# Final-norm column factors on VectorE instead of GpSimd, and a separate early buffer for the plain weights of the last product

## The chip, the cores and the metric

The kernel runs on one core of one Trainium2 chip. The metric is the device time of the whole program in microseconds (us), the median over several runs. A profile of one execution stands beside it; its span is the time from the first to the last instruction, and all moments named below are us from the start of that span.

## The reference, cut to what matters

One layer of a hybrid encoder on 528 tokens (512 real ones and 16 prepended) of width 2048, all in float32. `hn = rmsnorm(h) * g_in`; `P = hn @ w_in` (2048 x 8320); half of the columns feed an RWKV-7 recurrence, the other half a gated short convolution; the two results, 1024 wide each, are joined to `mix`. Then

```python
h_res = h_res + mix @ w_out[l]          # 512 x 2048 by 2048 x 2048
out = _rmsnorm(h_res, norm_f_g)         # h * rsqrt(mean(h*h) + eps) * norm_f_g
return out[:, N_META:]
```

The change lies wholly in these last lines: the product with `w_out`, the sum with `h_res`, and the final norm with its 2048 column factors `norm_f_g`.

## The kernel before, in words

**Numbers.** TensorE multiplies in a reduced float32 form, so each operand is split in two: ScalarE casts it to a high part (`hi`, L1215 for weights of the last stage), VectorE subtracts that from the plain value to get the low part (`lo`, L1216), and each product is the sum of three matmuls, `hi*hi`, `lo*hi` and `hi*lo`.

**Stages.** The first 842 us hold the input projection and the recurrence. Then TensorE runs the last stage, the product with `w_out`, and nothing else. The 2048 output columns are two halves of 1024, and each half is computed by a scheme with seven block products instead of eight: `M1`, `M2`, `P5`, `M7`, `M3`, `Q6`, `P4`. Sums of weight blocks and of activation blocks (`S1`, `S3`, `S4`, `S5`) are formed ahead of them, partly on VectorE (`add`, L1206; `sums`) and partly by transfers that add to what lies in memory (`add_by_transfer`, L1202, issued on GpSimd's queue). Each product is cut in four units g = 0 to 3 along the inner dimension; a unit is twelve matmuls of 128x512 (two token tiles, two inner slices, three matmuls each). The 56 units stand in the list `units`: `M1` and `M2` of the first half are units 0 to 7, its four blocks of `P5 M7 M3 Q6` are 8 to 23, then `P4` and the second half's `M1` up to 31, the second half's four blocks 32 to 47, its `P4` 48 to 51, its `M2` 52 to 55. The last four units, those of the second half's `M2`, run with the tail in a block of their own (the accumulators `end`).

**Order.** TensorE's order is written out. For the other engines, `at(u, fn, ...)` hangs a piece of work on unit u, and it is handed to the scheduler just before the matmuls of that unit; the scheduler then fixes each engine's own order, and every engine works its list strictly in that order. Only the tail block (from `row_part`) has VectorE, ScalarE and GpSimd in hand-written order. Buffers rotate: split weights `o` go through 6 half-unit slots (three units' worth), plain weights `wo` through 3 buffers (tag `raw`, loaded by `request`, L1148, on SyncE's queue SP), and a load into a buffer waits until its last reader is done. `x` are four standing buffers, one for each g, in which weight sums build up.

**After a product** comes `close`: VectorE adds the accumulators onto the output rows, which lie in `xa` (columns 0 to 1023) and `xb` (columns 1024 to 2047) on top of the residual (`onto`, L1224), and ScalarE squares the finished ones (`squares`, L1230).

**The two pieces that the change touches.** `gain` (L1299 to L1301) multiplies a finished 128x512 piece by its column factors, loaded to `gfb`. For columns 0 to 1023 that is eight pieces: four token tiles t, two column pieces n. They run on GpSimd, hung on units 30, 32, ..., 44. `load_home(g)` (L1304) fetches the plain weights of the second half's `M2`, unit g, through the three rotating `raw` buffers (hung on units 41, 43, 45, 47), and splits them into tiles called `home`, which lie where the activation sums `S` lay before. The mixed activations themselves (`mix`, four quarters with the tags `R0` to `R3`) are finished with once the sums are split; `R0` then takes `gfb`, `R2` and `R3` take `xb`, and `R1` stays unused.

Of the kernel before, what the change touches and what calls it, by code (L numbers as in the profile page):

```python
# [9 lines left out]
F32 = mybir.dt.float32  # L10
# [8 lines left out]
P = 128  # L19
# [58 lines left out]
def hymba_kernel(ctx: ExitStack, tc: tile.TileContext, xt, xtok, front, w_in, w_out, pv, lup, cst, msk, gf, out):  # L78
    nc = tc.nc
# [539 lines left out]
    def behind(dst, src):  # L619
        with tc.issue_after(state["dma"]):  # L620
            nc.sync.dma_start(dst, src)
# [450 lines left out]
    pp = ctx.enter_context(tc.tile_pool(name="pp", bufs=1, side="right", reuse_waits="tile"))  # L1072
# [70 lines left out]
    def rows_of(half, k, col, g):  # L1143
        return w_out[2 * half + col, 4 * k + g]

    def request(half, k, col, g):
        t = wp.tile([P, 1024], F32, tag="raw", name=f"wo{half}{k}{col}{g}", bufs=3)
        state["dma"] = nc.sync.dma_start(t, rows_of(half, k, col, g)).ins  # L1148
        straight[half, k, col, g] = t
# [58 lines left out]
    def split_unit(unit, t, home=None):  # L1208
        for q in range(2):
            rq = t()[:, q * 512 : (q + 1) * 512]  # L1210
            if home is None:
                hi, lo = slot(f"o{U[unit]}_{q}", OUT_AT)
            else:
                hi, lo = home[q]
            nc.scalar.copy(hi, rq)  # L1215
            nc.vector.tensor_tensor(out=lo, in0=rq, in1=hi.bitcast(F32), op=ALU.subtract)  # L1216
            right[unit, q] = (hi, lo)
# [64 lines left out]
    def at(u, fn, *args):  # L1282
        calls.setdefault(max(u, -1), []).append((fn, args))
# [17 lines left out]
        eng.tensor_tensor(out=h, in0=h, in1=gfs[0][:, n * 512 : (n + 1) * 512][:, o], op=ALU.mult)  # L1301


    def load_home(g):  # L1304
        request(1, 1, 0, g)
        f = ("S1", "S3", "S4", "S5")[g]
        tiles = [
            pw.tile([P, 4, HT], F32R, tag=f"{f}0{a}", name=f"home{g}{a}").rearrange("p a b -> p (a b)") for a in range(2)
        ]
        split_unit(  # L1310
            (1, "M2", g), passing(1, 1, 0, g),
            [(tiles[0][:, 512 * q : 512 * q + 512], tiles[1][:, 512 * q : 512 * q + 512]) for q in range(2)],
        )

    def passing(*block):
        return lambda: straight[block]

    def chained(g):
        return lambda: chain[g]
# [3 lines left out]
    for half in range(2):  # L1323
        for g in range(4):
            b, m1, m2 = U[half, "P5", g], U[half, "M1", g], U[half, "M2", g]
            if half:
                at(m1 - 4, begin_chain, 1, g)
                at(m1 - 2, split_unit, (1, "M1", g), chained(g))
            at(max(m1 + (half == 0 and g == 3), b - 5), add_by_transfer, half, 0, 1, g)
            at(b - (6 if g else 5), request, half, 0, 1, g)  # L1330
            at(b - (4 if g else 5), request, half, 1, 1, g)
            at(b - 2, split_unit, (half, "P5", g), chained(g))
            at(b - 1, add, passing(half, 0, 1, g), half, 1, 1, g)
            at(b - 1, split_unit, (half, "M7", g), passing(half, 0, 1, g))
            at(b, split_unit, (half, "M3", g), passing(half, 1, 1, g))
            at(b, add, chained(g), half, 1, 1, g)
            at(b + 1, split_unit, (half, "Q6", g), chained(g))
            at(b + 2, add_by_transfer, half, 1, 0, g)
            at(U[half, "P4", g] - 2, split_unit, (half, "P4", g), chained(g))
            if half:  # L1340
                at(m2 + 2 * g - g - 11, load_home, g)
            else:
                at(m2 - 5, request, 0, 1, 0, g)
                at(m2 - 2, split_unit, (0, "M2", g), passing(0, 1, 0, g))
# [6 lines left out]
    at(13, load_gain)  # L1351
    for m in range(2):
        at(21 + m, load_xb, m)
    for n in range(8):
        at(30 + 2 * n, gain, n // 2, n % 2, nc.gpsimd)

    for e in range(6):
        right[(0, "M1", e // 2), e % 2] = quarters[2 * N_IN + e]
# [5 lines left out]
    for u, unit in enumerate(units):  # L1364
        half, prod, g = unit
# [152 lines left out]
```

## Time and profile before

| | us |
|---|---|
| median of 3 runs (lowest, highest) | 1010.39 (1008.97, 1011.24) |
| the profiled execution | 1008.48 |
| its span | 1006.6 |
| last stage, from its first matmul on | 842.18 |
| first unit of the second half's blocks (`P5`, unit 32) starts | 929.07 |
| first matmul of the second half's `M2` (unit 52) starts | 987.03 |
| last matmul ends | 998.38 |

The profiled execution is 1.91 us below the median; of its own 1008.48 us, 1.9 lie outside the span. How to read the rows: PE is TensorE, DVE VectorE, ACT ScalarE, POOL GpSimd, and SPq, POOLq, ACTq their queues. A timeline row gives the start, the duration, the engine, the source line, the operation with output and inputs, and how many like it were merged (x4); in brackets the idle time just ahead of the row and what ended it. Consecutive instructions of one engine overlap by some 0.1 us, so of a merged row the duration divided by the count is the pace.

### The profile page before, as it was taken

The numbers are of one execution on the slowest core, as the hardware profiler recorded it, in microseconds if no ns is written. First come the engines' busy times: TensorE is split into PE (matmuls) and PEld (weight loads), VectorE is DVE, ScalarE is ACT, GpSimd is POOL, SyncE is SP. The second block draws the span as 40 slices with busy tenths as digits, with TensorE's granted clock in tenths as the row PEclk, the third lists the DMA queues.
The fourth block names the chain that finished last, engine by engine and source line by source line (L and its number), as shares of the span: only waits on it lengthen the run. The fifth ranks groups of instructions, "written<-read, shape, count | busy, mean of one in ns | idle before, by whom it ended". The sixth has DMA issues, their size and how long they took to land.

```text
span 1006.6 us, 23759 instructions
## 1 busy us (share of the span) xinstructions
PE 993.2 (99%) x9723; PEld 912.7 (91%) x9723; DVE 683.2 (68%) x1305; ACT 393.0 (39%) x729; POOL 288.0 (29%) x294
## 2 busy tenths in 40 slices
PE   9999999999999999999999999999999999999996
PEld 8999998999998999998999998889888898888775
DVE  7686955587765668654668654244555697999787
ACT  7553423344313434322434322222222336546453
POOL 0123313224223423232323222223332333047001
PEclk9999999999999999999999999999999999999998
DMA  9526476446674363854273856977673688796754
GB/s 338 155 70 154 115 205 159 125 125 146 155 186 146 94 171 99 218 152 119 85 175 94 222 141 192 340 237 234 216 216 95 177 271 235 210 281 146 173 130 168
DMA packets 185181, 175.35 MB, mean 174 GB/s; under 512 B 121584, under 2 KB 142832, under 8 KB 184560
## 3 DMA queue, kind: packets, MB, share of 16 engines
q1 hardware_dynamic: 182480, 164.92, 56.9%
q0 software_dynamic: 2304, 8.39, 4.9%
q8 instruction: 76, 1.25, 0.5%
q10 hardware_dynamic: 288, 0.52, 0.1%
q14 instruction: 33, 0.27, 0.1%
HBM read 137.44 MB, written 36.35 MB: 173 GB/s over the span
## 4 chain that ended last, share of the span: by engine, by line
PE 62%; DVE 5%; DMA 2%; issue 2%; ACT 0%; POOL 0%; DVEq 0%; ACTq 0%; POOLq 0%
PE ps_gc L328 8%; PE ps_B L328 7%; PE ps_h L328 7%; PE ps_C L328 7%; PE ps_k L328 5%; PE ps_v L328 5%; PE M L1243 5%; PE ps_g L328 5%; PE ps_r L328 5%; DVE o L1216 2%; PE P L1243 2%; DMA wo<-in_w_out_dram 2%; PE Q L1243 1%; PE zy L1010 1%; PE zs L1006 1%
## 5 line engine op out<-in xcount | busy, mean ns | idle before, releaser
L135 POOL TENSOR_TENSOR w<-wr,w 128x512 fp32r<-128x512 f32 x119 | 166.8, 1403 | 365.8 <-ACT w L134 317.5
L134 ACT CAST w<-wr 128x512 fp32r<-128x512 f32 x252 | 152.9, 618 | 280.9 <-PE ps_k L328 45.2
L135 DVE TENSOR_TENSOR w<-wr,w 128x512 fp32r<-128x512 f32 x133 | 95.9, 728 | 103.6 <-ACT w L134 93.3
L328 PE MATMUL ps_k<-xh,w 128*128 128x256 f32 (+1 forms) x512 | 95.7, 284 | 0.1
L328 PE MATMUL ps_r<-xh,w 128*128 128x256 f32 (+1 forms) x512 | 95.1, 281 | 0.0
L328 PE MATMUL ps_v<-xh,w 128*128 128x272 f32 (+1 forms) x512 | 95.0, 283 | 0.0
L328 PE MATMUL ps_h<-xh,w 128*128 128x258 f32 (+1 forms) x512 | 94.0, 282 | 0.0
L328 PE MATMUL ps_C<-xh,w 128*128 128x258 f32 (+1 forms) x512 | 93.2, 281 | 0.0
L328 PE MATMUL ps_g<-xh,w 128*128 128x258 f32 (+1 forms) x512 | 91.9, 281 | 0.0
L328 PE MATMUL ps_B<-xh,w 128*128 128x512 f32 x256 | 83.4, 395 | 0.1
L328 PE MATMUL ps_gc<-xh,w 128*128 128x512 f32 x256 | 81.7, 393 | 0.3 <-DVE w L135 0.3
L328 PEld LDWEIGHTS ps_h<-xh,w 128*128 128x128 f32 x512 | 79.7, 189 | 2.3 <-issue 1.6
L328 PEld LDWEIGHTS ps_k<-xh,w 128*128 128x128 f32 x512 | 80.3, 189 | 0.7 <-DVE w L135 0.3
L328 PEld LDWEIGHTS ps_r<-xh,w 128*128 128x128 f32 x512 | 80.3, 189 | 0.2
L328 PEld LDWEIGHTS ps_v<-xh,w 128*128 128x128 f32 x512 | 80.0, 189 | 0.3
L328 PEld LDWEIGHTS ps_C<-xh,w 128*128 128x128 f32 x512 | 79.6, 189 | 0.6
L328 PEld LDWEIGHTS ps_g<-xh,w 128*128 128x128 f32 x512 | 79.3, 189 | 0.4
L328 PE MATMUL ps_k<-xl,w 128*128 128x272 f32 (+1 forms) x256 | 72.9, 285 | 0.0
L328 PE MATMUL ps_v<-xl,w 128*128 128x256 f32 (+1 forms) x256 | 72.5, 283 | 0.0
L328 PE MATMUL ps_r<-xl,w 128*128 128x256 f32 (+1 forms) x256 | 72.4, 283 | 0.0
L328 PE MATMUL ps_g<-xl,w 128*128 128x256 f32 (+1 forms) x256 | 72.3, 282 | 0.0
L328 PE MATMUL ps_C<-xl,w 128*128 128x256 f32 (+1 forms) x256 | 71.9, 281 | 0.0
(320 smaller groups left out, 2288.2 us busy)
## 6 DMA issues: line engine op xcount, KB each, us to landing
wr<-in_w_in_dram SPq DMA_DIRECT2D x126, 512.0 KB
ct<-opd SPq DMA_DIRECT2D x64, 288.0 KB
wo<-in_w_out_dram SPq DMA_DIRECT2D x25, 512.0 KB
x<-in_w_out_dram POOLq DMA_DIRECT2D x16, 512.0 KB, 5.7
opd<-ar SPq DMA_DIRECT2D x8, 576.0 KB
opd<-gt SPq DMA_DIRECT2D x16, 288.0 KB
opd<-bt SPq DMA_DIRECT2D x64, 64.0 KB
x<-in_w_out_dram SPq DMA_DIRECT2D x8, 512.0 KB
```

The lines of the kernel that those rows point to most:

```text
L134: nc.scalar.copy(hi, rq)
L135: low[q] = eng.tensor_tensor(out=lo, in0=rq, in1=hi.bitcast(F32), op=ALU.subtract).ins
L328: nc.tensor.matmul(ps[r], ww[:, w], xx[:, kt, a:b], start=(kt == 0 and n == 0), stop=(kt == KT - 1 and n == 2))
L1006: nc.tensor.matmul(d[hs, j], w, x[hs], start=(a == 0), stop=(a == b - 1))
L1010: nc.tensor.matmul(d[ho, j], t[hs, o : o + CH], x[hs], start=(a == 0), stop=(a == b - 1))
L1216: nc.vector.tensor_tensor(out=lo, in0=rq, in1=hi.bitcast(F32), op=ALU.subtract)
L1243: nc.tensor.matmul(bank[s], left(prod, jj, m, s), w, start=(jj == 0 and n == 0), stop=(jj == 7 and n == 2))
```

## The change

The eight `gain` calls go to VectorE and are hung on units 34, 35, 38, 39, 41, 42, 44 and 46. The plain weights of the second half's `M2` no longer pass through the rotating `raw` buffers: `fetch_home(0)` loads those of g = 0 and 1 into the unused quarter `R1` (hung on unit 23), `fetch_home(1)` those of g = 2 and 3 into the same quarter (hung on unit 44, and so once the first pair is split). `load_home` only splits; it is hung on units 40, 43, 47 and 48 instead of 41, 43, 45 and 47.

```diff
+    plain = {}
+
+    def fetch_home(pair):
+        t = pp.tile([P, 4, 512], F32, tag="R1", name=f"plain{pair}").rearrange("p a b -> p (a b)")
+        for g in (2 * pair, 2 * pair + 1):
+            plain[g] = t[:, g % 2 * 1024 : g % 2 * 1024 + 1024]
+            behind(plain[g], rows_of(1, 1, 0, g))
+
     def load_home(g):
-        request(1, 1, 0, g)
         f = ("S1", "S3", "S4", "S5")[g]
         tiles = [
             pw.tile([P, 4, HT], F32R, tag=f"{f}0{a}", name=f"home{g}{a}").rearrange("p a b -> p (a b)") for a in range(2)
         ]
         split_unit(
-            (1, "M2", g), passing(1, 1, 0, g),
+            (1, "M2", g), lambda: plain[g],
             [(tiles[0][:, 512 * q : 512 * q + 512], tiles[1][:, 512 * q : 512 * q + 512]) for q in range(2)],
         )
...
             if half:
-                at(m2 + 2 * g - g - 11, load_home, g)
+                at((40, 43, 47, 48)[g], load_home, g)
...
+    at(23, fetch_home, 0)
+    at(44, fetch_home, 1)
     for n in range(8):
-        at(30 + 2 * n, gain, n // 2, n % 2, nc.gpsimd)
+        at((34, 35, 38, 39, 41, 42, 44, 46)[n], gain, n // 2, n % 2, nc.vector)
```

In the built program, TensorE's list is the same. On VectorE the scheduler puts two of the eight gains ahead of the splits of unit 19, one between the splits of units 30 and 31, two behind those of unit 31, one behind those of unit 32, and the last two ahead of those of unit 35; the addition of two `wo` buffers that stood ahead of unit 35's splits now stands behind them. The `home` splits stand, half by half, between the splits of units 39, 40 and 41 (g = 0 and 1) and of units 43 to 46 (g = 2 and 3). Behind the last unit's splits, the four pairs of small sums over the squares (`row_part`) stand ahead of the last two additions of `P4` instead of behind them. GpSimd's list loses the eight gains and keeps its transfers in their order. On SP the first pair's two loads stand right behind those of `xb`, and the second pair's two loads are the last before the outputs.

## Prediction

> **What bounds the kernel now.** I read the chain of waits first, because it says which engine holds the end, then TensorE's timeline in the last stage, then that of the engine it waits for.
>
> ```profile
> span 1006.6 us, 23759 instructions
> ```
> ```profile
> 842.18 21.77 PE M L1243 x96
> ...
> 925.38 4.46 DVE o L1216
> ...
> 961.51 5.53 DMA wo<-in_w_out_dram
> ```
>
> Up to 918 us the chain names almost only PE, so nothing there can be won by moving work of other engines. One number is needed from it: 96 matmuls without a stop take 21.77 us, so a unit of twelve takes 2.721. Behind that the chain leaves PE for splits on VectorE (one of 4.46 us) and for weight loads. TensorE's timeline shows what these cost:
>
> ```profile
> 929.07 2.92 PE L1243 MATMUL P<-o,S 128*128 128x512 f32 x12
> ...
> 933.16 5.55 PE L1243 MATMUL M<-o,S 128*128 128x512 f32 x23 [0.95 <-DVE o L1216]
> ...
> 939.28 2.77 PE L1243 MATMUL Q<-o,S 128*128 128x512 f32 x11 [0.35 <-DVE o L1216]
> 941.89 2.88 PE L1243 MATMUL P<-o,S 128*128 128x512 f32 x12
> ...
> 969.67 2.82 PE L1243 MATMUL M<-o,S 128*128 128x512 f32 x11 [0.19 <-DVE o L1216]
> ...
> 981.68 5.51 PE L1243 MATMUL P<-o,m 128*128 128x512 f32 x23 [0.28 <-DVE o L1216]
> 987.03 5.60 PE L1243 MATMUL end<-home,m 128*128 128x512 f32 x24
> ```
>
> Four stops, each released by a low part `o` from VectorE. The brackets understate them, because a stop also loses the overlap of matmuls; the starts give the whole loss. Units 32 to 35 take 941.89 - 929.07 = 12.82 us instead of 4 x 2.721 = 10.88: 1.94 lost. Units 36 to 51 take 987.03 - 941.89 = 45.14 instead of 43.54: 1.60 lost. So 3.54 us is what this stage can give back.
>
> **Part 1, the eight gains.** What they do now, on GpSimd, and what VectorE does meanwhile:
>
> ```profile
> 883.93 8.89 POOL L1301 TENSOR_TENSOR xa<-xa,gfb 128x512 f32<-128x512 f32 x2 [0.52 <-DMA gfb<-in_gf_dram]
> ...
> 925.47 1.59 POOL L1301 TENSOR_TENSOR xa<-xa,gfb 128x512 f32<-128x512 f32 x1
> ...
> 927.32 1.90 POOL L1301 TENSOR_TENSOR xa<-xa,gfb 128x512 f32<-128x512 f32 x1
> ...
> 929.18 2.23 POOL L1301 TENSOR_TENSOR xa<-xa,gfb 128x512 f32<-128x512 f32 x1
> ...
> 940.24 0.90 POOL L1202 DMA_DIRECT2D x<-in_w_out_dram  x1 [8.82 <-DVE o L1216]
> ```
> ```profile
> 889.13 1.29 DVE L1216 TENSOR_TENSOR o<-x,o 128x512 fp32r<-128x512 f32 x2
> ...
> 917.91 1.22 DVE L1206 TENSOR_TENSOR wo<-wo,wo 128x1024 f32<-128x1024 f32 x1
> ...
> 924.00 5.83 DVE L1216 TENSOR_TENSOR o<-x,o 128x512 fp32r<-128x512 f32 x2 [0.25 <-ACT o L1215]
> 929.86 2.64 DVE L1206 TENSOR_TENSOR x<-x,wo 128x1024 f32<-128x1024 f32 x1
> 932.43 1.28 DVE L1216 TENSOR_TENSOR o<-wo,o 128x512 fp32r<-128x512 f32 x2
> ...
> 937.40 1.23 DVE L1206 TENSOR_TENSOR wo<-wo,wo 128x1024 f32<-128x1024 f32 x1 [1.29 <-DMA wo<-in_w_out_dram]
> 938.54 2.50 DVE L1216 TENSOR_TENSOR o<-x,o 128x512 fp32r<-128x512 f32 x4
> ...
> 995.54 0.68 DVE L1301 TENSOR_TENSOR xb<-xb,gfb 128x512 f32<-128x512 f32 x1
> ```
>
> A pair of splits takes 1.29 us at 889.13; the pair at 924.00 takes 5.83, just while three gains run on GpSimd. The addition at 929.86 takes 2.64 where the one at 917.91 takes 1.22. Excess 4.54 + 1.42 = 5.96 us. The next split, unit 33's (932.43), is the one TensorE stops for at 933.16.
>
> The Trainium skill ("SBUF — State Buffer", Who interferes with whom) says that a VectorE operation with two inputs in SBUF and a GpSimd operation that reads SBUF exclude each other for whole instructions. By it VectorE would have waited at most for the three gains, 1.59 + 1.90 + 2.23 = 5.72 us, beside 5.96 by VectorE's own rows; the sum comes out alike.
>
> Added on VectorE: the same operation stands there already, 0.68 us alone, and four in a row go at 2.50 / 4 = 0.62. Four of the gains now stand between the splits of unit 30 and those of unit 33: 4 x 0.62 = 2.48. So unit 33's splits start 5.96 - 2.48 = 3.5 us earlier, at about 928.9, and TensorE wants the low part at 929.07 + 2.72 + 0.23 = 932.0: it is there by 929.6, and the stop goes. If the contention were halved only, 3.0 - 2.5 would still bring it 0.5 earlier and leave about 0.6 of the stop. The last two gains stand ahead of unit 35's splits. These stop TensorE at 939.28 today, because VectorE first waits for a load until 937.40 for an addition; that addition now stands behind them, so 1.24 us of gains replace 2.4 us of waiting and adding, on a list that is 3.5 us early. Both stops of this stretch go: **-1.94**, bounds 0 and -1.94.
>
> The first two gains stand ahead of unit 19's splits, at 889.13 today. Their factors were there at 883.93, when GpSimd started on them, so VectorE doesn't wait. 1.24 us later unit 19's splits end at 891.7; TensorE starts that unit at 842.18 + 19 x 2.721 = 893.9. Cost nothing, hidden by these 2 us. GpSimd's transfers no longer queue behind gains, and come earlier; who waits for them is not late now, so no gain.
>
> **Part 2, the plain weights.** What VectorE and ScalarE do ahead of the two late stops:
>
> ```profile
> 967.06 1.14 ACT L1215 CAST home<-wo 128x512 fp32r<-128x512 f32 x2 [4.31 <-DMA wo<-in_w_out_dram]
> ...
> 979.20 1.14 ACT L1215 CAST o<-x 128x512 fp32r<-128x512 f32 x2 [2.37 <-DMA x<-in_w_out_dram]
> ```
> ```profile
> 967.72 1.29 DVE L1216 TENSOR_TENSOR home<-wo,home 128x512 fp32r<-128x512 f32 x2 [2.57 <-ACT home L1215]
> 968.93 1.29 DVE L1216 TENSOR_TENSOR o<-wo,o 128x512 fp32r<-128x512 f32 x2
> ...
> 977.34 1.29 DVE L1216 TENSOR_TENSOR home<-wo,home 128x512 fp32r<-128x512 f32 x2
> 978.55 2.47 DVE L1224 TENSOR_TENSOR xb<-xb,M 128x512 f32<-128x512 f32 x4
> 980.94 1.29 DVE L1216 TENSOR_TENSOR o<-x,o 128x512 fp32r<-128x512 f32 x2
> ```
> ```profile
> 942.00:962.00 20.00, 20.00 (x90) 16.58 (x89) 14.22 (x22) 9.35 (x17) 1.74 (x2) 1.00 0.60 156
> ...
> 976.00:987.00 11.00, 10.71 (x47) 8.55 (x46) 11.00 (x20) 1.97 (x4) 0.00 (x0) 1.00 0.20 38
> ```
>
> In the windows VectorE (third busy column) is idle for 5.8 of the 20 us from 942 on, and never from 976 to 987. A `home` load that came late held ScalarE 4.31 us and VectorE 2.57, and unit 46's split at 968.93, the stop at 969.67, waited behind them. The stop at 981.68 is unit 50's split at 980.94, behind the `home` pair at 977.34 and four additions. Now the first pair of loads is in memory long before, and all four `home` splits stand ahead of unit 46's last ones: VectorE does 4 x 1.24 us of them by about 963, in the stretch where it was idle. Behind 967 it has three pairs, 3.7 us, less to do, against losses of 1.60: **-1.60**, bounds 0 and -1.60.
>
> Two loads move past others on SP. The first pair, 1 MB, comes ahead of `wo` loads of the second half:
>
> ```profile
> 889.50 0.77 SPq L1148 DMA_DIRECT2D wo<-in_w_out_dram  x1
> ```
>
> At the 390 GB/s that the output rows below show, 1 MB delays what is behind it by 2.7 us; its first reader is the addition at 917.91, 28 us later. Nothing. The second pair needs its quarter free (g = 1 split, about 949) and the `wo` load ahead of it on SP issued, which waits for unit 41's splits, done at the latest when TensorE starts that unit: 929.07 + 9 x 2.721 = 953.6. With the slow 5.53 us load of the chain and 2 x 1.35 (0.52 MB at 390 GB/s) for the two behind it, the last lands at 961.8. ScalarE has its cast ahead of unit 45's, wanted at 929.07 + 13 x 2.721 = 964.4, less two casts of 0.6: 963.2. Hidden by 1.4 us in this worst count.
>
> **Part 3, the tail.** Reordered row sums: the four pairs now wait on ScalarE's squares ahead of the last two additions, but at a moment when VectorE has caught up, so nothing. Beside that:
>
> ```profile
> 993.06 0.34 SPq L1405 DMA_DIRECT2D out_dram<-xb  x1
> ```
> ```profile
> GB/s 0 0 0 0 0 0 0 0 0 289 429 410 386 366 395 376 386 366 419 429 414 366 424 424 347 400 371 376 390 362 400 376 386 386 198 19 0 0 0 0
> ```
>
> The second row covers 990 to 1007 in steps of 0.425 us: from the first output on, the transfers run full, some 390 GB/s, for 11 us until 1005. The first output starts when VectorE is done with all additions, 3.5 us behind the end of `P4` at 987; with VectorE no longer behind, it starts up to 2.5 us earlier against TensorE, and the last rows, released by TensorE's end, find a shorter queue. Between 0 and -0.5; I take **-0.3**.
>
> Sum: -1.94 - 1.60 - 0.3 = -3.84. Against the profiled execution, 1008.48, that gives 1004.6; the median of the runs shown is 1010.39, so 1006.5.
>
> **Rivals.**
>
> *Only the first stops go* (0.13). VectorE stays saturated behind 967, or the late stops come from the additions alone. For it: 11.00 busy of 11.00. Against: 3.7 us of `home` splits leave that stretch. -1.94: 1008.4.
>
> *The gains are not what slows VectorE* (0.06), but GpSimd's three transfer issues between them. Then the 5.96 stays and 2.48 comes on top; the stop at 939 (0.4) and the late ones (1.6) still go: +0.5, 1010.9. Against: the issue at 940.24 falls into the four splits at 938.54, which keep their 0.62.
>
> *The second pair lands late* (0.06), the case for slower. Place: ScalarE's cast ahead of unit 45's. From 963.2 on each us of lateness stops TensorE for one. If its loads went one behind the other at 5.53 each, the last would land at 953.6 + 16.6 = 970.2: +7.0 - 3.84 = +3.2, 1013.6. Against: full rate is 1.35 a load.
>
> *Accumulating transfers starve* (0.03). The last one for `P4`:
>
> ```profile
> 973.63 0.88 POOL L1202 DMA_DIRECT2D x<-in_w_out_dram  x1 [12.24 <-DVE o L1216]
> ...
> DMA to landing us min/median/max: 5.3/5.6/9.3
> ```
>
> If its issue had to wait for a pause in a VectorE that is now busy without one until about 982, it would land 5.6 later at 987.6; with cast and split at 988.8, for unit 51 at 929.07 + 19 x 2.721 = 980.8: +8.0 - 3.84 = +4.2, 1014.6. Against: issued at 973.63, it had landed at 979.20, in the middle of a busy VectorE.
> The Trainium skill ("SBUF — State Buffer", SBUF: two separate sides) describes such a starving of transfers issued on GpSimd by VectorE operations in a 2-port mode; by these rows it does not happen under this kernel's two-input ones.
>
> **How the numbers follow.** The forecast has 0.72. Range 1005.0 to 1010.0: below, -4.04 and the 1.4 by which the lowest run lies under the median; above, the first rival and that spread; left out are the last three, 0.15. Faster means by over 0.2% (2 us), about what a measurement of this kernel can tell from no change: forecast without its weak edge and half of the first rival, 0.74; within 0.2%: 0.17; slower: 0.09.
>
> **What would show it.** Right: splits of units 32 and 33 at 0.6 to 0.7 us each, no DVE release in PE's rows behind 929, `end` starting near 983.5, the first output near 987 to 990, no ScalarE wait on `home` loads. Wrong: a split of over 1 us with GpSimd idle; PE waiting at units 45 or 51 (late load, starved transfer); or all stops gone and the end not moved, if the outputs bound it.

## The result and the profile after

| | before | after |
|---|---|---|
| median (lowest to highest) of 8 runs, us | 1010.72 (1008.97 to 1013.59) | 1005.67 (1004.08 to 1009.29) |
| profiled execution, us | 1008.48 | 1006.95 |
| its span | 1006.6 | 1005.2 |
| last stage starts | 842.02 | 842.72 |
| unit 32 starts | 929.07 | 931.77 |
| tail block (`end`) starts | 987.03 | 986.17 |

The stage's first matmul row starts at 842.02; the 842.18 given ahead of the prediction is where the chain of waits enters the stage. The ratio is 0.9952, 95% interval [0.9937, 0.9966]: 5.05 us by the medians, against 3.84 forecast. The profiled execution of the changed kernel is 1.28 us above its own median, and its span is only 1.4 us shorter. So this one profile needs care. TensorE's timeline, from the first unit at which it stops, to the tail (start, duration, instruction, count, idle time before it and its releaser):

```profile
868.50 5.52 PE L1243 MATMUL M<-o,S 128*128 128x512 f32 x23 [0.43 <-DVE o L1216]
...
880.18 5.51 PE L1243 MATMUL M<-o,S 128*128 128x512 f32 x23 [0.16 <-DVE o L1216]
...
931.77 2.88 PE L1243 MATMUL P<-o,S 128*128 128x512 f32 x12
...
975.29 11.04 PE L1243 MATMUL P<-o,m 128*128 128x512 f32 x48
986.17 5.60 PE L1243 MATMUL end<-home,m 128*128 128x512 f32 x24
```

From unit 32 to the tail no bracket is left: 986.17 - 931.77 = 54.40 us for twenty units of 2.720, where the kernel before took 57.96. All 3.54 us that the forecast had counted there are gone. But two stops stand near units 9 and 13 (868.50 and 880.18), where instructions and order are the same in both kernels, and with them the first 32 units take 931.77 - 842.72 = 89.05 us instead of the 87.05 of before: 2.0 us of the gain are hidden in this execution. They come back below.

VectorE at the place of the old contention, and GpSimd there:

```profile
927.75 1.28 DVE L1301 TENSOR_TENSOR xa<-xa,gfb 128x512 f32<-128x512 f32 x2
928.95 1.28 DVE L1216 TENSOR_TENSOR o<-x,o 128x512 fp32r<-128x512 f32 x2
930.16 0.68 DVE L1301 TENSOR_TENSOR xa<-xa,gfb 128x512 f32<-128x512 f32 x1
930.76 1.22 DVE L1206 TENSOR_TENSOR x<-x,wo 128x1024 f32<-128x1024 f32 x1
931.89 1.28 DVE L1216 TENSOR_TENSOR o<-wo,o 128x512 fp32r<-128x512 f32 x2
```
```profile
928.23 0.89 POOL L1202 DMA_DIRECT2D x<-in_w_out_dram  x1 [2.13 <-DVE o L1216]
```

Pairs of splits take 1.28 us again, where a pair had taken 5.83, and a multiplication takes 0.68 alone and 0.64 in a pair. GpSimd's transfer issues still fall between them (928.23) and slow nothing. The long split of before, 4.46 us at 925.38, is one of 0.68 plus 3.78, and the two GpSimd multiplications that ran beside it took 1.59 + 1.90 = 3.49 by their rows. The Trainium skill ("SBUF — State Buffer", Who interferes with whom) says that the side which has the shared ports keeps them for its whole instruction, and that the other blocks fully meanwhile; the trace agrees to 0.3 us.

The `home` splits, and one wait that the forecast had not seen, on ScalarE:

```profile
914.52 2.19 ACT L1215 CAST o<-x 128x512 fp32r<-128x512 f32 x4 [3.69 <-DMA x<-in_w_out_dram]
...
960.03 0.62 ACT L1215 CAST home<-plain 128x512 fp32r<-128x512 f32 x1 [2.90 <-DMA plain<-in_w_out_dram]
```

The second pair landed at 960.0, when ScalarE had waited 2.90 us for it; VectorE's `home` halves, which stand between the splits of units 43, 44 and 45, follow at once, and no stop comes of it. The first pair's 1 MB pushed an `x` load of unit 27 back, so that its cast waited 3.69 us; TensorE did not stop for it. One window (its length, then busy us and count of PE, PEld, DVE, ACT, POOL):

```profile
962.00:976.00 14.00, 14.00 (x64) 11.58 (x63) 14.00 (x23) 8.21 (x15) 0.88 (x1) 1.00 0.47 70
```

VectorE is busy without a pause from 962 to 976, PE too: a full VectorE that is ahead costs nothing. The accumulating transfers did not starve under it:

```profile
DMA to landing us min/median/max: 5.1/5.8/9.8
```

### The profile page after: what moved, and what is told of

Its sections match the earlier page's. It is cut to its first block, busy times and chain, and to the rows that moved or that the text cites. A ratio compares the mean times of both kernels' runs of the same rounds, so it can differ in the third digit from the quotient of the medians.

```text
span 1005.2 us, 23750 instructions
## 1 busy us (share of the span) xinstructions
PE 993.7 (99%) x9723; PEld 913.6 (91%) x9723; DVE 680.5 (68%) x1313; ACT 393.2 (39%) x729; POOL 264.2 (26%) x286
## 3 DMA queue, kind: packets, MB, share of 16 engines
q8 instruction: 76, 1.25, 0.5%
## 4 chain that ended last, share of the span: by engine, by line
PE 65%; DVE 3%; DMA 1%; ACT 1%; SPq 0%; issue 0%; DVEq 0%; POOL 0%; ACTq 0%
PE ps_gc L328 8%; PE ps_B L328 7%; PE ps_h L328 7%; PE ps_C L328 6%; PE M L1243 5%; PE ps_k L328 5%; PE ps_v L328 5%; PE ps_g L328 5%; PE ps_r L328 5%; PE P L1243 4%; PE Q L1243 2%; PE zy L1010 1%; PE zs L1006 1%; PE g L681 1%; PE rz L954 1%; DVE o L1216 1%
```

## The experiments

All were measured against runs of the kernel before on the same chip. **Lost** below is read from each TensorE timeline: start of `end` less the first matmul of the last stage, less 141.46, which is the shortest such stretch (the changed kernel profiled again, 984.43 - 842.97). "Tail" is the span less the start of `end`.

| kernel | median us | ratio, 95% interval | lost up to unit 31 | lost in 32 to 51 | tail |
|---|---|---|---|---|---|
| before, first profile | | | 0 | 3.55 | 19.57 |
| whole, first profile | 1005.67 | 0.9952 [0.9937, 0.9966] | 1.99 | 0 | 19.03 |
| gains alone | 1005.43 | 0.9955 [0.9937, 0.9972] | 0 | 0.05 | 19.05 |
| homes alone | 1008.35 | 0.9981 [0.9969, 0.9993] | 2.06 | 1.40 | 19.37 |
| gains left out | 1006.53 | 0.9966 [0.9953, 0.9979] | 0.33 | 0.02 | 19.48 |
| whole, again | 1005.04 | 0.9949 [0.9934, 0.9965] | 0 | 0 | 18.97 |
| gains alone, doubled | 1006.45 | 0.9970 [0.9958, 0.9982] | 0 | 0.73 | 19.10 |
| whole, first pair later | 1004.78 | 0.9955 [0.9938, 0.9972] | 0.42 | 0 | 19.01 |
| whole, residual later | 1005.79 | 0.9962 [0.9948, 0.9976] | 0.42 | 0.02 | 19.24 |
| gains alone, residual later | 1005.48 | 0.9957 [0.9941, 0.9973] | 0 | 0 | 19.07 |
| whole, gains doubled | 1004.56 | 0.9944 [0.9929, 0.9960] | 0 | 0 | 19.02 |

### The two parts, each alone

The theory was the forecast's: two causes, one for each part. Its rival: one cause, GpSimd's multiplications, whose lateness is carried on to the late stops.

Gains alone is the kernel before with one edit:

```diff
-        at(30 + 2 * n, gain, n // 2, n % 2, nc.gpsimd)
+        at((34, 35, 38, 39, 41, 42, 44, 46)[n], gain, n // 2, n % 2, nc.vector)
```

> Only the eight column factors go to VectorE; the weights of the last product come through the rotating buffers as before. Theory (two separate causes): the two stops near 933 and 939 go, worth 1.9 us, the stops near 970 and 982 stay within 0.5 us of their 1.6: -1.5 to -2.5 us against the kernel before. Rival (one cause: VectorE, once ahead, stays ahead, and the late loads matter no more): all stops go, -3.5 to -5 us, as the whole change. Rival (VectorE is full and the gains only add to it): 0 or slower.

Measured: 1005.43 against 1009.49, 4.1 us by the medians and 4.5 by the ratio, nearly all of the whole change. TensorE's timeline of gains alone:

```profile
929.50 2.88 PE L1243 MATMUL P<-o,S 128*128 128x512 f32 x12
...
973.01 11.10 PE L1243 MATMUL P<-o,m 128*128 128x512 f32 x48
983.95 5.60 PE L1243 MATMUL end<-home,m 128*128 128x512 f32 x24
```

The stops of before at 969.67 and 981.68 are gone too, although the `home` weights still go through the rotating buffers. Only the 11.10 us of the last `P4`, 0.06 more than in the whole change, are left of them. The one-cause rival holds, and the theory falls.

Homes alone is the other part, with the gains left on GpSimd:

```diff
-        at((34, 35, 38, 39, 41, 42, 44, 46)[n], gain, n // 2, n % 2, nc.vector)
+        at(30 + 2 * n, gain, n // 2, n % 2, nc.gpsimd)
```

> Only the separate buffer and the earlier splits of the last product's weights; the eight column factors stay on GpSimd at their old places. Theory: the long split near 924 (5.8 us for two) and the stops near 933 and 939 stay, the two late stops go, and the first output leaves earlier: -1.5 to -2.2 us against before. Rival (one cause, the gains): nothing, within 0.7 us of before. Rival (the moved splits press on VectorE while GpSimd still holds it back): slower by 0.5 to 1.5 us.

Measured: 1008.35, by the ratio 1.9 us (0.7 to 3.1) below before, as the theory had it, but only 1.1 by the medians; its profile, of 1008.30 us, does not bear the theory's reason out. TensorE's timeline of homes alone, and ScalarE's cast ahead of the last stop:

```profile
925.40 3.73 PE L1243 MATMUL M<-o,m 128*128 128x512 f32 x15 [0.71 <-DVE o L1216]
...
929.35 2.14 PE L1243 MATMUL M<-o,m 128*128 128x512 f32 x8 [0.22 <-DVE o L1216]
931.33 2.89 PE L1243 MATMUL P<-o,S 128*128 128x512 f32 x12
...
965.85 2.11 PE L1243 MATMUL P<-o,S 128*128 128x512 f32 x8 [0.24 <-DVE o L1216]
```
```profile
962.65 0.62 ACT L1215 CAST home<-plain 128x512 fp32r<-128x512 f32 x1 [5.79 <-DMA plain<-in_w_out_dram]
```

The contention struck here before unit 32 and cost 2.06 us there, then 1.40 more, of which 1.24 from unit 44 on. The stops of before at units 46 and 50 are gone, but a new one stands in unit 44: VectorE does its split behind a `home` split of the second pair, and that pair landed only at 962.6. So the forecast's rival *The second pair lands late* came true in this kernel, by a stop. All in all it lost 3.46 us in this execution, hardly less than the 3.55 of before; where the 1.1 to 1.9 us come from, one profile doesn't show.

### Multiplications or transfer issues

Gains left out is the kernel before without its eight multiplications (so columns 0 to 1023 lack their factor), with all of GpSimd's transfers:

```diff
-    for n in range(8):
-        at(30 + 2 * n, gain, n // 2, n % 2, nc.gpsimd)
```

> The kernel before without the eight column factors at all (columns 0 to 1023 of the output lack the factor, so this is no result, only a time). Theory (GpSimd's multiplications hold VectorE's two-input operations): splits of units 32 and 33 take 0.6 to 0.7 us each, the stops near 933 and 939 go, and it comes within 0.5 us of the kernel that has only the gains moved, as VectorE's 2.5 us for them are hidden. Rival (GpSimd's three transfer issues in that stretch hold VectorE): the 5.8 us pair stays, no gain against before.

Measured: 54.42 us from unit 32 to the tail and no stop there. TensorE and VectorE of this kernel, where the pair of splits had taken 5.83:

```profile
929.60 2.88 PE L1243 MATMUL P<-o,S 128*128 128x512 f32 x12
...
984.02 5.60 PE L1243 MATMUL end<-home,m 128*128 128x512 f32 x24
```
```profile
924.33 1.38 DVE L1216 TENSOR_TENSOR o<-x,o 128x512 fp32r<-128x512 f32 x2 [0.83 <-ACT o L1215]
```

From 886 to 985 the operations of VectorE and of ScalarE come in the same order as in the kernel before. So the multiplications were the cause, of the late stops too, and the transfer issues were not. The median, 1006.53, is 1.1 above gains alone, not within 0.5 as expected, though the intervals overlap. Eight multiplications on VectorE cost nothing that can be seen.

The whole change once more beside these:

> The whole change once more beside its parts, on the same chip. Theory: no stop of TensorE behind unit 30, -3.8 to -5 us against before, and the sum of the two parts within 1 us. Rival (parts overlap): the whole is no better than the better part.

Measured: 1005.04, 4.45 below before. Its profiled execution took 1005.19. From that of before: 0.95 later start of the stage, 3.55 not lost, 0.60 less tail, 1008.48 + 0.95 - 3.55 - 0.60 = 1005.28. Whether the parts add up the times can't tell: alone they give 6.4 by the ratios beside 5.1 for both, over 1 us more, but 5.2 beside 4.45 by the medians. What can be said is that the whole change is not measurably better than gains alone (0.9949 and 0.9955), as the rival had it, and that by the profiles gains alone leave 0.05 us to win.

### Is VectorE full, and what does the separate buffer buy?

Each gain done twice (columns 0 to 1023 get the factor squared) adds 8 x 0.62 us on VectorE, first without the buffer:

```diff
+        for _ in range(2):
-        at((34, 35, 38, 39, 41, 42, 44, 46)[n], gain, n // 2, n % 2, nc.vector)
+            at((34, 35, 38, 39, 41, 42, 44, 46)[n], gain, n // 2, n % 2, nc.vector)
```

> Gains on VectorE without the separate buffer, and each of the eight multiplications done twice, so that columns 0 to 1023 carry the factor squared: eight more VectorE operations of 0.62 us, 4.96 us in all, with nothing on GpSimd. Of them some six stand between the splits of units 30 and 35. Theory, that a VectorE held up by GpSimd lost TensorE's time once and that the late stops were the same lateness carried on: in e1 the splits of unit 33 had about 1.8 us to spare; the second copies take up to 2.5 us there, so a stop of 0 to 0.7 us comes back near 932, well under the 1.94 of before, and what is late is made up in the 5.8 idle us of 942 to 962, so no late stop over 0.2 us. Against e1: 0 to +0.8 us. Rival, that VectorE is simply full in this stage and any addition moves the end by its length: +3 to +5 us against e1, with late stops as in the kernel before.

Measured: 1.0 us above gains alone by the medians, 1.5 by the ratios, a little more than the theory had, and 0.73 lost. The rival's 3 to 5 us did not come, so VectorE is not full; but the theory had the place wrong, and its "no late stop over 0.2 us" failed. The scheduler put the extra copies near unit 20 and behind unit 36's splits, so the stretch ahead of unit 33 wasn't loaded, and the stop came at unit 50. TensorE and VectorE of this kernel:

```profile
973.79 5.98 PE L1243 MATMUL P<-o,m 128*128 128x512 f32 x25
980.03 5.53 PE L1243 MATMUL P<-o,m 128*128 128x512 f32 x23 [0.26 <-DVE o L1216]
```
```profile
975.69 1.29 DVE L1216 TENSOR_TENSOR home<-wo,home 128x512 fp32r<-128x512 f32 x2
976.89 2.48 DVE L1224 TENSOR_TENSOR xb<-xb,M 128x512 f32<-128x512 f32 x4
979.28 1.30 DVE L1216 TENSOR_TENSOR o<-x,o 128x512 fp32r<-128x512 f32 x2
```

In gains alone that split starts at 977.74, and its first half is done 0.3 us before TensorE wants it (929.50 + 18 x 2.72 + 0.23 = 978.7). The separate buffer should turn this 0.3 into several us. The same doubling in the changed kernel:

> The whole change with each of the eight multiplications done twice, as in e5 (columns 0 to 1023 carry the factor squared). e5, without the separate buffer, lost 0.7 us between unit 32 and the tail, with a stop at unit 50, whose split was 0.3 us ahead of TensorE in e1 and 3.5 us ahead in the changed kernel. Theory, that the separate buffer buys time in hand at units 46 and 50, which is worth something only where VectorE is late: no stop behind unit 32, start of unit 32 to the start of the tail within 0.1 us of 54.42, and the time within 0.7 us of the changed kernel's, so 0.5 to 1.5 us below e5. Rival, that it buys nothing: the stop at unit 50 comes back and the time is e5's.

Measured: 1004.56 and nothing lost; 984.58 - 930.18 = 54.40. That is 1.9 us below the same doubling without the buffer, by the medians, more than the 0.5 to 1.5 expected; the lost 0.73 explains a part, and the rest stays open. TensorE's timeline and VectorE's split of unit 50:

```profile
930.18 2.88 PE L1243 MATMUL P<-o,S 128*128 128x512 f32 x12
...
973.70 11.04 PE L1243 MATMUL P<-o,m 128*128 128x512 f32 x48
984.58 5.60 PE L1243 MATMUL end<-home,m 128*128 128x512 f32 x24
```
```profile
973.93 1.32 DVE L1216 TENSOR_TENSOR o<-x,o 128x512 fp32r<-128x512 f32 x2
```

The first half is done at 974.6, wanted at 979.4: 4.8 us in hand. By one profile of each, part 2 buys time in hand that the gains alone don't need, but that twice the gains do.

### The first pair's traffic, and the early stops

The first pair of plain weights at unit 32 instead of 23:

```diff
-    at(23, fetch_home, 0)
+    at(32, fetch_home, 0)
```

> The whole change, with the first pair of plain weights fetched at unit 32 instead of 23. In the changed kernel its 1 MB stands ahead of three wo loads and four x loads of the second half, and one x cast waited 3.69 us for its load near 914, though TensorE did not stop there. Theory, that this delay is hidden: the wait of the cast goes, TensorE's rows stay without stops behind unit 26, and the time is within 0.7 us of the changed kernel. Rival, that the earlier lateness costs what VectorE later lacks: 1 us or more faster. Rival, that the pair now lands too late for the home casts of units 40 and 43: stops there and 1 us or more slower.

Measured: ScalarE's wait for the `x` load is gone, nothing is lost behind unit 31, and the ratio, 0.9955, can't be told from that of the changed kernel. The delay was hidden.

The residual loads, and the additions of the first `M1`, later:

```diff
-        at((0, 1, 8, 9)[t], load_xa, t)
+        at((4, 4, 8, 9)[t], load_xa, t)
...
-            at(u + LATE.get(prod, 1), close, half, prod, z[prod])
+            at(u + (4 if (half, prod) == (0, "M1") else LATE.get(prod, 1)), close, half, prod, z[prod])
```

> The whole change, with the first two residual loads into xa hung on unit 4 instead of 0 and 1, and the additions of the first half's M1 two units later, so that four wo loads of the first half go ahead of them on SP. In the profiled run of the changed kernel TensorE stopped at 868.5 and 880.2 and lost about 1.8 us between units 8 and 14, behind a wo load of 8.1 us; the other profiles show 0 to 0.4 there. Theory, that those stops come and go from run to run with the load's time and have no part in the change: with the loads earlier they are gone in this profile, the median falls by 0 to 0.8 us against the changed kernel and the spread of the runs is smaller. Rival, that they are tied to the separate buffer: they stay. Rival, that the later additions make VectorE late near unit 6 to 10: a stop there of up to 1 us and as much slower.

> Gains on VectorE without the separate buffer, and the residual loads later as in e7. Theory: within 0.7 us of e7, since with the gains off GpSimd the separate buffer was worth nothing that could be told apart, and -4 to -5.5 us against the kernel before. Rival, that the separate buffer does pay once the early stops are gone: 1 us or more slower than e7.

Measured: 1005.79 on the whole change and 1005.48 on gains alone, no gain over the kernels without the edit. The two lie within 0.7 us of each other, as the theory had it, but the early loss isn't gone: 0.42 us still went at unit 13 in the first of them, as in the kernel with the first pair later, which has the old loads. What can be said of these early losses: they appear in kernels of either kind (0.33 in gains left out, 1.2 in one execution of before, below) and are absent in gains alone and in the whole change again, so nothing here ties them to the change. In the profiled execution of the changed kernel they stand behind one long load, by the chain of waits:

```profile
851.89 8.10 DMA wo<-in_w_out_dram
860.09 0.63 ACT o L1215
```

Why a load takes 8.10 us in one execution stays open.

### The kernel before, profiled three more times

By the medians the change gave more than the 3.84 forecast from one profile. Does the loss of before vary?

> The kernel before, unchanged, for one more profile. Its profiled execution shown here (1008.48 us) is one of its faster ones; its median is 1.2 to 2.2 us above it, while e1 and e4 lie within 0.4 us of their profiles. The forecast summed -3.84 against that profile, the medians gave -5.05. Theory, that the loss to GpSimd's multiplications differs from execution to execution: in a run of 1010 us or more units 32 to 51 lose 4.5 to 6 us instead of 3.54, by larger or more stops. Rival, that the slower runs start the last stage later or stop in units 0 to 31, as the profiled run of the changed kernel did: 3.5 us as before in units 32 to 51, and the rest ahead of 929.

> The kernel before, unchanged, for a third profile. As for the second: 4.5 to 6 us lost in units 32 to 51 in a run of 1010 us or more if the loss to GpSimd's multiplications varies, 3.5 us there and the rest ahead of unit 32 if the slower runs lose their time elsewhere.

> The kernel before, unchanged, for a fourth profile, with the same two readings as for the second and third.

| execution of before | us | lost up to unit 31 | lost in 32 to 51 | time less both |
|---|---|---|---|---|
| first | 1008.48 | 0 | 3.55 | 1004.9 |
| second | 1008.90 | 1.25 | 2.42 | 1005.2 |
| third | 1011.39 | 1.21 | 4.94 | 1005.2 |
| fourth | 1009.82 | 0 | 4.20 | 1005.6 |

The last column moves by 0.7 us only, and it is about the changed kernel's time. So the loss differs from execution to execution, 3.55 to 6.15 us. In the third, the only one of the four above 1010 us, units 32 to 51 lose 4.94, as the theory had it; its other 1.21 fell earlier, as the rival had it. That 1.21 is not GpSimd's: it lies between 866 and 880, and the first multiplication starts at 886.02; it is one of the early losses above. The second's 1.25 lies at 924 and 928, beside the multiplications. So what the multiplications cost ran from 3.55 to 4.94, and the forecast had read the smallest of the four (3.55, 3.67, 4.94, 4.20). In TensorE's timeline of the third, two of the stops of the first stand again, and a stop behind a late cast on ScalarE besides:

```profile
935.23 5.55 PE L1243 MATMUL M<-o,S 128*128 128x512 f32 x23 [0.92 <-DVE o L1216]
...
971.78 0.50 PE L1243 MATMUL M<-o,S 128*128 128x512 f32 x1 [0.46 <-ACT o L1215]
972.67 2.77 PE L1243 MATMUL M<-o,S 128*128 128x512 f32 x11 [0.39 <-DVE o L1216]
```

## Why the prediction was right, and where it was wrong

**Part 1, right.** The splits are at pace, unit 33's start at 931.89, 0.1 us behind the start of unit 32 (forecast: 0.2 us ahead of it), and the stops of units 33 and 35 are gone. With the gains left out they go as well, so the price put on them, nothing beside the contention, holds; and since the addition that waited until 937.40 keeps its place there, the second stop needed no new order, only the lateness gone. *The gains are not what slows VectorE* is refuted by that run.

**Part 2, wrong in its cause.** The step that failed is "Behind 967 it has three pairs, 3.7 us, less to do, against losses of 1.60: -1.60". In gains alone VectorE still does those three pairs behind 964, and the 1.60 is won back all the same; in homes alone they all but leave that stretch, and 1.24 is lost from unit 44 on even so. The error lay in a row read the wrong way: VectorE was "idle for 5.8 of the 20 us from 942 on", and that was taken for room. The waits between 929 and 987 (engine, line waited for: us in all, times, longest) tell what the idle time was. Before, then gains alone:

```profile
ACT home L1215 <- DMA wo<-in_w_out_dram: 8.7, 3, 4.3
DVE wo L1206 <- DMA wo<-in_w_out_dram: 7.0, 3, 3.0
```
```profile
ACT home L1215 <- DMA wo<-in_w_out_dram: 7.4, 3, 3.6
...
DVE wo L1206 <- DMA wo<-in_w_out_dram: 2.4, 2, 1.4
```

VectorE was waiting for loads: its waits before the additions at 947.36 (2.65) and 957.68 (3.02) make up 5.67 of the 5.8. ScalarE's waits for `home` loads hardly shrink, 8.7 to 7.4, though the stops go; on a list that is ahead they do no harm. A load into one of the three `raw` buffers starts when the split of its last reader is done, so a VectorE that is late at 925 starts loads late, and they make it late again at the next turn. The chain of waits of before says so from the long split on:

```profile
925.38 4.46 DVE o L1216
...
933.74 3.64 DMA wo<-in_w_out_dram
...
954.69 4.82 DMA wo<-in_w_out_dram
...
961.51 5.53 DMA wo<-in_w_out_dram
967.06 0.63 ACT home L1215
...
967.72 1.29 DVE home L1216 x2
```

The first turn can be seen in gains left out. There, in the same order, the load that stands at 933.74 in this chain is issued 5.3 us earlier, and the addition of 937.40 follows it as much earlier. SP's queue and VectorE in gains left out:

```profile
928.46 0.33 SPq L1148 DMA_DIRECT2D wo<-in_w_out_dram  x1
```
```profile
932.09 1.23 DVE L1206 TENSOR_TENSOR wo<-wo,wo 128x1024 f32<-128x1024 f32 x1 [0.35 <-DMA wo<-in_w_out_dram]
```

The late stops were the first lateness, carried on for 45 us. That they hang on it is shown by gains alone and by gains left out; that it is these buffers that carry it to the end, and no other way, is argued from the chain. The sum came out, but partly by luck: the 1.60 was earned by part 1, and the parts were priced as if they added. *Only the first stops go* (0.13) rested on the same reading: in no run without gains on GpSimd did the first stops go and the late ones stay; the 0.73 of the doubled gains came of added work.

**The loads.** "28 us later. Nothing" named the wrong reader: the `x` load behind the first pair was late, by 3.69 us of ScalarE's waiting. It was hidden, as the later fetch shows. The second pair landed at 960.0; the worst count, 961.8, was made on a clock that ran 2.7 us earlier. But its place, ScalarE's cast ahead of unit 45's, was not the tight one, and the sign "no ScalarE wait on `home` loads" did not hold: ScalarE waited 2.90 us. Behind it VectorE does the splits of units 44 and 45 with no pause; the second half of unit 44's is done at 963.2 and wanted at 964.41 + 4 x 0.227 = 965.3, the first half of unit 45's at 965.5, wanted at 967.4. So there were about 2 us in hand. *The second pair lands late* did not happen in the changed kernel, but it did in homes alone, at unit 44. *Accumulating transfers starve* did not happen (5.1/5.8/9.8).

**The tail**, forecast -0.3: -0.5 in the first profile of the change and -0.6 in the second. The reason given does not hold. First output of the changed kernel, and the DMA view's rates from 990 to 1007:

```profile
989.38 0.34 SPq L1414 DMA_DIRECT2D out_dram<-xb  x1
```
```profile
GB/s 178 376 439 386 414 357 318 265 337 24 294 333 0 424 414 386 10 67 386 414 390 371 386 386 68 72 405 342 395 381 381 381 111 0 0 0 0 0 0 0
```

The outputs start 3.2 us behind the start of `end` instead of 6.0, 2.8 earlier (forecast: up to 2.5), and the transfers now pause (24, 0, 10). But in gains alone they start at +5.9, and the tail is as short, 19.05; with the gains left out they start at +6.0, and it is 19.48. Before and after the change the last output is issued 14.8 us behind `end` (1001.81 - 987.03 and 1000.96 - 986.17), and only its way to the end of the span shrinks, from 4.8 to 4.2. What shortens it stays open.

**The size.** Forecast 3.84 from a profile of before that lost 3.55; without the third's early 1.21, the four profiles lost 4.1 on average, and the tail gave 0.5 to 0.6: an estimate of 4.6 to 4.7, beside 5.05 and 4.45 measured by medians.

## What to carry to other kernels

Idle time of an engine is room only if it doesn't end in a wait for something that the engine itself released late: look at what ended each pause before you count it as slack, and follow a late load back to the reader that freed its buffer. Where several edits each remove the same lateness, price them together, or measure them alone; a buffer that only adds time in hand shows its worth when load is added. One profile of a kernel with contention is one draw: its loss here ran from 3.55 to 4.94 us over four executions.

## What the runs showed of the hardware

VectorE and GpSimd, both with two-input 128x512 operations, hit each other differently in two executions of the same program. At 914 the first execution of before let VectorE through and stretched GpSimd:

```profile
914.30 2.50 DVE L1224 TENSOR_TENSOR xa<-xa,sh 128x512 f32<-128x512 f32 x4
```
```profile
914.28 10.62 POOL L1301 TENSOR_TENSOR xa<-xa,gfb 128x512 f32<-128x512 f32 x3 [1.02 <-ACT sqj_None L1230]
```

The second did the reverse:

```profile
914.43 4.69 DVE L1224 TENSOR_TENSOR xa<-xa,sh 128x512 f32<-128x512 f32 x4
```
```profile
914.49 1.77 POOL L1301 TENSOR_TENSOR xa<-xa,gfb 128x512 f32<-128x512 f32 x1 [1.14 <-ACT sqj_None L1230]
```

In the first, three multiplications took 10.62 us while four additions kept their 0.62; in the second, one multiplication took 1.77 and the four additions 4.69, and TensorE's stops came ahead of unit 32 (1.25 us lost there). So which side waits differs between executions of one program, with starts that differ by a tenth of a microsecond. The Trainium skill ("SBUF — State Buffer", Who interferes with whom) has it that issue order decides who blocks. By the starts of these rows it would be the other way about: GpSimd's row begins 0.02 us ahead of VectorE's where GpSimd was stretched, and 0.06 behind it where VectorE was. But the starts don't decide either: GpSimd began 0.28 ahead in the third execution (916.10 and 916.38) and was stretched, to 10.87 us for three, and 0.27 ahead in homes alone (914.90 and 915.17), where VectorE was, to 4.69 for four. Spans on GpSimd are rough, so this is left open; no run here tells what decides.
